# Block products for two more pairs of the second down projection, and DRAM sums for four more units of the second up projection

## The chip, the cores and the metric

The kernel runs on one core of a Trainium2 chip. A core has five engines with queues of their own: TensorE (PE; its weight loads are listed as PEld), VectorE (DVE), ScalarE (ACT), GpSimd (POOL) and SyncE (SP), and 16 DMA engines that all of them feed. The metric is the device time of one execution in microseconds, the median of several runs. Before the change it is 1062.77 us (three runs, 1062.4 to 1063.34).

## The reference

One macaron layer on 512 tokens of 1024 channels, all in float32:

```python
def swiglu(x, w_gate, w_up, w_down):
    return (jax.nn.silu(x @ w_gate) * (x @ w_up)) @ w_down
...
        x = x + 0.5 * swiglu(rmsnorm(x, ffn1_norm[l]), ffn1_wg[l], ffn1_wu[l], ffn1_wd[l])
        x = x + hybrid_mixer(rmsnorm(x, mix_norm[l]), w_in[l], conv_w[l], conv_b[l],
                             rg_wa[l], rg_ba[l], rg_wx[l], rg_bx[l], rg_lam[l],
                             w_att_proj[l], w_rnn_proj[l], w_out[l])
        x = x + 0.5 * swiglu(rmsnorm(x, ffn2_norm[l]), ffn2_wg[l], ffn2_wu[l], ffn2_wd[l])
    return rmsnorm(x, final_norm)
```

The inner width of both feed-forward layers is 2816, that is 22 tiles of 128 rows. The mixer holds sparse attention and a recurrent branch; the change leaves its arithmetic alone.

## The kernel before

**Split precision.** A float32 matrix product is made of three TensorE products: each operand is split into a rounded high part and a remainder (`wsplit`, L238: ACT writes `wh`, DVE writes `wl` as the difference), and high by high, high by low and low by high are added up in PSUM. Nearly every instruction is recorded through one helper, so the profile gives L171 for all of them; tiles tell them apart.

**Stages in order of time.** First up projection, first down projection, mixer (64 jobs of the list `ORDER`, placed by a planner with costs and due times), second up projection, second down projection with the final norm. The two feed-forward stages stand in an order that is written out by hand: events with due times, then a stream of steps.

**Block products.** Two tiles of weights make a two by two block matrix with blocks a11, a12, a21, a22, and seven block products replace eight. They need the sums s1 = a21+a22, s3 = a21+a11, s2 = s1+a11 and s4 = s2+a12 of the weights; the products are numbered 1 (a11), 2 (a12), 3 (s4), 4 (a22), 5 (s1), 6 (s2), 7 (s3). The signs stand in the other operand.

**Second up projection** (`ffn_up`, called with `blocks=BLOCKS2U`). Four tiles of gate and up weights (`DIRECT2`) are multiplied plainly, in eight direct products. The other 18 tiles are 18 units w of seven products each, 126 steps in `stream`. Step i is emitted as `products(i)`, then `step(i)`, which splits the weights of step i+4 (`prepare`, `LEAD` = 4) and reads the results of step i-1. A unit of the plain kind loads its blocks into SBUF slots (`load`), forms s1 and s3 by accumulating DMAs of the POOL queue and s2 and s4 by DVE additions. A unit with an entry in `BLOCKS2U` reads blocks and sums from DRAM: `fetch_pair` loads the weights of two steps into one of three buffers (`RAWS` = 3, tile `wr`). Its sums were formed in DRAM by eight copies and accumulating copies of the POOL queue (class `Blocks`, `stages`). Units 6 to 17 are of this kind (`UNITS` = 6), and all of their seven products are wide: the high weights meet high and low part of the other operand in one 512 column matmul, and one of 256 columns adds the low weights; the halves of the sum are added when the result is read (`copies`, `reads`). Units 0 to 5 have products 2, 5 and 3 wide (`WIDE`), the other four take three matmuls of 256 columns.

**Pace of the DRAM sums.** The sums of the second down projection (`sum_groups`, L1516) are issued between the first mixer jobs, up to the job `SUMS_FROM`; from that job on `sums_until` (L1069) issues those of the second up projection. At each call it records a small DVE `memset` and a POOL copy of it (tile `beat`), so that the POOL queue does not run ahead of DVE. `SUMS_PART` of these moves go out in the mixer, `DIRECT_PART` beside the direct products, the rest over the first `SUMS_STEPS` steps of the stream.

**Second down projection** (`block_down` with its own loop). The 22 hidden tiles are `hs`: the first `PLAIN` = 6 are multiplied plainly, the others form `PAIRS` = 8 pairs (a, b). A step ("D", h, k) multiplies plain tile k for output half h (12 matmuls of 512 columns), a step (p, j) is product p of pair j (6 matmuls of 512 columns). The order of the 68 steps: the six D steps of half 0, products 1, 2, 5 for all pairs, then 6 and 3 with four D steps of half 1 between them, 7, two D steps, 4. Tasks are keyed to steps: the weights of two steps are split four steps ahead (`split_pair`, three `wh`/`wl` buffers), an operand (tile `cm`, two halves) is made some 5 or 6 steps ahead, and `differences(j)` (DVE: tile `cr`, and `h` in place) stands at step j. Tasks of negative steps run beside the last steps of the stream (`ahead`). At steps 0 to 3 `turn` transposes the residual (8 small matmuls each, and four ACT copies to tile `xr`). The results of the D steps of half 0 are added to `xr` by four DVE instructions after step 5.

Of the kernel before, what the change touches and what calls it, by code (L numbers as in the profile page):

```python
# [14 lines left out]
P = 128  # L15
# [161 lines left out]
def hybrid_kernel(ctx, tc, xt, vec, w1u, w1d, wm, wki, wrg, watt, wrnn, wout, w2u, w2d, gf, out):  # L177
# [243 lines left out]

    def ffn_up(y, wu, n0, tiles, hs, g, norm, norm_at, waiting=(), given=(), ahead=None, blocks={}, wide=()):

# [312 lines left out]
        if ahead and waiting:  # L736
            def held(d):
                nc.vector.memset(beat[:, d:d + 1], 0.0)
                nc.gpsimd.tensor_copy(beat[:, d:d + 1], beat[:, d:d + 1])
                ahead(d - 200)  # L740

            for d in range(PAIRS // 2 + 1):
                at(R + 0.7 + 5.4 * d, held, d)
# [30 lines left out]
        with tc.manual_schedule(engines=ENGINES):  # L774
# [9 lines left out]
            for i in range(len(stream)):  # L784
                begin(T0 + i * 1.42)
                products(i)
                step(i)
                if ahead:
                    ahead(i - len(stream))
                if i % 14 == 12 and i // 14 < PLAIN:  # L790
                    halve(hs, i // 14)
                if blocks and i % 2 == 0:
                    sums_until(SUMS_PART + DIRECT_PART + (1 - SUMS_PART - DIRECT_PART) * min(1.0, i / SUMS_STEPS))
                if i % 7 == 1 and loaded[0] < count - len(blocks):
                    load_ = load()
                next(load_, None)
# [12 lines left out]

    def down_blocks(wd):  # L810
        part = lambda b, j: wd[b * (PAIRS // 2) + j // 2][:, j % 2 * S:(j % 2 + 1) * S]
        return [Blocks(*(part(b, j) for b in range(4))) for j in range(PAIRS)]

    def block_down(hs, wd, sums, blocks=None):

# [17 lines left out]
        def block(b, j):  # L833

            i, half = b * (PAIRS // 2) + j // 2, j % 2 * S
            return wd[i][:, half:half + S]
# [3 lines left out]
        def source(i):  # L840
            if steps[i][0] == "D":
                _, h, k = steps[i]
                return wd[2 * PAIRS + h * (PLAIN // 2) + k // 2][:, k % 2 * S:(k % 2 + 1) * S]
            p, j = steps[i]
# [26 lines left out]

        a = lambda j: hs[PLAIN + 2 * j]
        b = lambda j: hs[PLAIN + 2 * j + 1]

# [40 lines left out]
        for i, st in enumerate(steps):  # L915
# [8 lines left out]
            if st[0] == "D":  # L924
                _, h, k = st
                key = ("D", h, k // 2)
                if k % 2 == 0:
                    used.append([i - 4, index["D", h, k + 1] - 4, key, 2 * PAIRS + h * (PLAIN // 2) + k // 2])
                task(i - 4, unit(i, lambda key=key, k=k: raws[key][:, k % 2 * S:(k % 2 + 1) * S]))
                continue  # L930
            p, j = st
            if p in (1, 4, 2):
                key = (p, j // 2)
                if j % 2 == 0:
                    used.append([i - 4, index[p, j + 1] - 4, key, {1: 0, 2: 1, 4: 3}[p] * (PAIRS // 2) + j // 2])
                src = lambda key=key, j=j: raws[key][:, j % 2 * S:(j % 2 + 1) * S]
# [53 lines left out]

        d.steps, d.index, d.tasks, d.tasks_at, d.units, d.turned = steps, index, tasks, tasks_at, units, turned
        return d
# [173 lines left out]
    def products1(i, ms=range(KD // 2)):  # L1166
        h, l = (t[:, i % 2 * S:(i % 2 + 1) * S] for t in d1.units[i // 2])
        if steps[i][0] == "D":
            _, half, k = steps[i]
            hh, hl = hs[k]  # L1170
            for m in ms:
# [4 lines left out]
                T.matmul(o, h[:, c], hl, start=False, stop=False)  # L1176
                T.matmul(o, l[:, c], hh, start=False, stop=k == PLAIN - 1)
            return
        p, j = steps[i]
        t = d1.turned[p, j]  # L1180
        for m in ms:
# [4 lines left out]
            T.matmul(o, h[:, c], t[:, hi], start=False, stop=False, **opens)  # L1186
            T.matmul(o, l[:, c], t[:, lo], start=False, stop=j == PAIRS - 1, **opens)

# [4 lines left out]
    def results1(i):  # L1193
        st = steps[i]
        if st[0] == "D":
            if st[2] == PLAIN - 1:
# [3 lines left out]
        elif st[1] == PAIRS - 1:  # L1200
            for a in ADDS[st[0]]:
# [683 lines left out]
    def products(i, ms=range(2)):  # L1885
        h, l = (t[:, i % 2 * S:(i % 2 + 1) * S] for t in units[i // 2])
        if steps[i][0] == "D":
            _, half, k = steps[i]
            hh, hl = hs[k]
            for m in range(NQ):  # L1890
# [135 lines left out]
def _layout(i):  # L2026
    def blocks(d):

        t = d[0].reshape(KF, P, 2, S)
        pairs = t[PLAIN:].reshape(PAIRS // 2, 2, 2, P, 2, S).transpose(4, 2, 0, 3, 1, 5).reshape(2 * PAIRS, P, 2 * S)  # L2030
        plain = t[:PLAIN].reshape(PLAIN // 2, 2, P, 2, S).transpose(3, 0, 2, 1, 4).reshape(PLAIN, P, 2 * S)
        return np.concatenate([pairs, plain])
# [5 lines left out]
    for n, g in enumerate(("rg_wa", "rg_wx")):  # L2038
# [35 lines left out]
```

## Time and profile before

| | |
|---|---|
| median of three runs | 1062.77 us |
| profiled execution | 1061.5 us |
| its span, first to last instruction | 1059.7 us |
| direct products of the second up projection | about 716 to 762 us |
| its stream of 126 steps | 762.4 to 940.0 us |
| second down projection | 940.0 to about 1052 us, then the last norm and stores |

Times within the span count from its first instruction. In rows of the timeline the columns are start, duration, engine, line, operation, tiles as out<-in, shape and count; in brackets stands the idle time before and what ended it. Matmuls overlap in the array, so the pace of PE is read from the difference of starts and not from durations; the same holds for DVE, where the next instruction starts some 0.09 us before the one ahead of it ends.

### The profile page before, as it was taken

The numbers are of one execution on the slowest core, as the hardware profiler recorded it, in microseconds if no ns is written. First come the engines' busy times: TensorE is split into PE (matmuls) and PEld (weight loads), VectorE is DVE, ScalarE is ACT, GpSimd is POOL, SyncE is SP. The second block draws the span as 40 slices with busy tenths as digits, with TensorE's granted clock in tenths as the row PEclk, the third lists the DMA queues.
The fourth block names the chain that finished last, engine by engine and source line by source line (L and its number), as shares of the span: only waits on it lengthen the run. The fifth ranks groups of instructions, "written<-read, shape, count | busy, mean of one in ns | idle before, by whom it ended". The sixth has DMA issues, their size and how long they took to land.

```text
span 1059.7 us, 16590 instructions
## 1 busy us (share of the span) xinstructions
PE 1051.1 (99%) x5716; PEld 909.6 (86%) x5716; DVE 884.9 (84%) x1742; ACT 667.1 (63%) x1250; POOL 237.2 (22%) x357
## 2 busy tenths in 40 slices
PE   9999999999999999999999999999999999999997
PEld 7889999989999788888888888888899888888885
DVE  6679999989988879999899866865799888878875
ACT  7456656656476657976886664445666666666663
POOL 0261323302131011212031444442732000000020
PEclk9999999999999999999999999999999999999999
DMA  9786999938783477667494878999994666545573
GB/s 326 180 170 159 264 225 231 233 97 236 182 220 122 128 225 171 179 181 188 126 234 123 208 177 198 278 236 261 265 223 100 191 197 197 180 155 167 187 205 122
DMA packets 94548, 205.26 MB, mean 194 GB/s; under 512 B 11776, under 2 KB 18560, under 8 KB 93824
## 3 DMA queue, kind: packets, MB, share of 16 engines
q1 hardware_dynamic: 60720, 136.24, 39.2%
q0 software_dynamic: 33024, 67.13, 32.9%
q8 instruction: 45, 0.74, 0.3%
q10 hardware_dynamic: 720, 0.84, 0.2%
q14 instruction: 39, 0.32, 0.1%
HBM read 194.72 MB, written 48.23 MB: 229 GB/s over the span
## 4 chain that ended last, share of the span: by engine, by line
PE 97%; ACT 1%; DVE 1%; DMA 0%; issue 0%
PE mm L171 68%; PE aux L171 29%; DMA vt<-vec 0%; ACT L171 0%; ACT rl L171 0%; ACT r L171 0%; DVE tu L171 0%; DVE o L171 0%; DVE wl L171 0%; ACT wh L171 0%; DVE tg L171 0%; ACT yh L171 0%; DVE xr L171 0%; DVE sq L171 0%; ACT xc L171 0%
## 5 line engine op out<-in xcount | busy, mean ns | idle before, releaser
L171 DVE TENSOR_TENSOR wl<-wr,wh 128x1024 fp32r<-128x1024 f32 (+2 forms) x233 | 232.2, 1000 | 60.5 <-ACT wh L171 58.8
L171 ACT ACTIVATE wh<-wr 128x1024 fp32r<-128x1024 f32 (+3 forms) x235 | 203.7, 873 | 76.4 <-PE aux L171 24.0
L171 PE MATMUL mm<-cm,wh 128*128 128x256 f32 (+1 forms) x1184 | 240.9, 310 | 0.0
L171 PEld LDWEIGHTS mm<-cm,wh 128*128 128x128 f32 x1184 | 189.3, 191 | 7.3 <-ACT tu L171 0.2
L171 PE MATMUL mm<-cm,wl 128*128 128x256 f32 x736 | 172.5, 282 | 0.0
L171 PE MATMUL mm<-yh,wh 128*128 128x512 f32 (+1 forms) x416 | 163.8, 394 | 0.3 <-ACT i L171 0.2
L171 PE MATMUL mm<-yl,wh 128*128 128x512 f32 (+1 forms) x416 | 162.2, 390 | 0.0
L171 PE MATMUL mm<-yh,wl 128*128 128x512 f32 x408 | 159.2, 390 | 0.0
L171 PEld LDWEIGHTS mm<-cm,wl 128*128 128x128 f32 x736 | 130.0, 190 | 6.1
L171 PE MATMUL aux<-cm,wh 128*128 128x512 f32 (+1 forms) x472 | 122.9, 379 | 0.0
L171 PEld LDWEIGHTS mm<-yh,wh 128*128 128x128 f32 (+1 forms) x416 | 78.0, 187 | 17.1 <-ACT i L171 0.6
L171 PEld LDWEIGHTS mm<-yl,wh 128*128 128x128 f32 (+1 forms) x416 | 77.6, 187 | 15.6 <-DVE yl L171 0.5
L171 PEld LDWEIGHTS mm<-yh,wl 128*128 128x128 f32 x408 | 76.6, 188 | 16.4 <-DVE wl L171 0.2
L171 PEld LDWEIGHTS aux<-cm,wh 128*128 128x128 f32 x472 | 79.7, 189 | 9.4
L171 ACT ACTIVATE wh<-s 128x512 fp32r<-128x512 f32 x96 | 58.8, 625 | 43.3 <-DVE s L171 32.9
L171 DVE TENSOR_TENSOR wl<-s,wh 128x512 fp32r<-128x512 f32 x96 | 65.4, 688 | 14.5 <-ACT wh L171 13.8
L171 PEld LDWEIGHTS aux<-cm,wl 128*128 128x128 f32 x440 | 68.8, 189 | 8.7
L171 PE MATMUL aux<-cm,wl 128*128 128x256 f32 x440 | 74.0, 281 | 0.0
L326 POOL DMA_DIRECT2D scr<-w2d x32 | 29.6, 1003 | 175.5 <-DMA scr<-w2d 163.5
L159 POOL DMA_DIRECT2D s<-w1u x44 | 41.3, 1136 | 114.4 <-DVE wl L171 69.7
L159 POOL DMA_DIRECT2D cm<-h x16 | 13.8, 863 | 207.5 <-ACT cm L171 198.0
L171 PE MATMUL mm<-wh,cm 128*128 128x512 f32 x192 | 59.1, 389 | 0.0
(267 smaller groups left out, 2151.6 us busy)
## 6 DMA issues: line engine op xcount, KB each, us to landing
wr<-scr SPq DMA_DIRECT2D x80, 256.0 KB, 2.9
wr<-wm SPq DMA_DIRECT2D x39, 512.0 KB, 3.9
scr<-w2u POOLq DMA_DIRECT2D x72, 256.0 KB, 6.1
s<-w1u POOLq DMA_DIRECT2D x44, 256.0 KB, 7.6
scr<-scr POOLq DMA_DIRECT2D x40, 256.0 KB, 6.1
wr<-w1u SPq DMA_DIRECT2D x19, 512.0 KB, 6.2
wr<-w1d SPq DMA_DIRECT2D x18, 512.0 KB, 4.2
wr<-w2u SPq DMA_DIRECT2D x36, 256.0 KB, 2.9
```

The lines of the kernel that those rows point to most:

```text
L159: return self.engine.dma_start(out, src, **kw)
L171: return call(*args, **kw)
L326: plain, adds = nc.gpsimd.dma_start, lambda o, i: nc.gpsimd.dma_start(o, i, accum_op=ALU.add)
```

## The change

The constants of the second feed-forward layer part from those of the first.

- `PLAIN2` = 2 and `PAIRS2` = 10 in the second down projection: four of the six plain tiles become two more pairs, so that 74 steps replace 68. No D step of half 1 stands between products 6 and 3 any more; both stand ahead of product 4.
- `UNITS` = 2: units 2 to 5 of the second up projection read their sums from DRAM and become all wide.
- The pace of the sums: 128 moves in place of 96 for the up projection and 80 in place of 64 for the down projection; they begin at job 33 in place of 37, 68% of them go in the mixer, 7% beside the direct products, and the remaining 32 moves over the first 62 steps (before 9 or 10 over 44).

```diff
-PLAIN, PAIRS, TAIL = 6, 8, 3
+PLAIN1, PAIRS1, PLAIN2, PAIRS2, TAIL = 6, 8, 2, 10, 3
...
-UNITS, SUMS_FROM, SUMS_PART, DIRECT_PART, SUMS_STEPS, SUMS_TIME = 6, 37, 0.8, 0.1, 44, 145
+UNITS, SUMS_FROM, SUMS_PART, DIRECT_PART, SUMS_STEPS, SUMS_TIME = 2, 33, 0.68, 0.07, 62, 185
...
-                if i % 14 == 12 and i // 14 < PLAIN:
+                if i % 14 == 12 and i // 14 < halves:
                     halve(hs, i // 14)
...
-        steps = [("D", 0, k) for k in range(PLAIN)] + [(p, j) for p in (1, 2, 5) for j in range(PAIRS)]
+        steps = [("D", 0, k) for k in range(plain)] + [(p, j) for p in (1, 2, 5) for j in range(pairs)]
         for p in (6, 3):
-            for j in range(PAIRS):
-                steps += [(p, j)] + [("D", 1, (6, 3).index(p) * 2 + j // 3)] * (j in (2, 5))
-        steps += [(7, j) for j in range(PAIRS)] + [("D", 1, k) for k in (4, 5)] + [(4, j) for j in range(PAIRS)]
+            for j in range(pairs):
+                steps += [(p, j)] + [("D", 1, (6, 3).index(p) * 2 + j // 3)] * (j in (2, 5) and plain > 2)
+        steps += [(7, j) for j in range(pairs)] + [("D", 1, k) for k in range(plain - 2, plain)] + [(4, j) for j in range(pairs)]
...
-    d2 = block_down(hs, w2d, x, BLOCKS2D)
+    d2 = block_down(hs, w2d, x, PLAIN2, PAIRS2, BLOCKS2D)
...
-    ffn_up(y2, w2u, 0, DIRECT2, hs, V_G2, norm_steps(acc), (2.73, 3.2, 3.4, 4.78, 5.3), ahead=tasks_at, blocks=BLOCKS2U, wide=WIDE)
+    ffn_up(y2, w2u, 0, DIRECT2, hs, PLAIN2, V_G2, norm_steps(acc), (2.73, 3.2, 3.4, 4.78, 5.3), ahead=tasks_at, blocks=BLOCKS2U, wide=WIDE)
```

The other lines hand these numbers on (`PLAIN1` and `PAIRS1` for the first layer, whose values stay 6 and 8) and lay the weights out to match.

On DVE, at the front of the second down projection, from the four results of the plain steps on (tile `xr`). Before:

```order
L171 SCALAR_TENSOR_TENSOR xr_10544<-aux_10560,xr_10544 128x512
L171 SCALAR_TENSOR_TENSOR xr_10544<-aux_10564,xr_10544 128x512
L171 SCALAR_TENSOR_TENSOR xr_10545<-aux_10568,xr_10545 128x512
L171 SCALAR_TENSOR_TENSOR xr_10545<-aux_10572,xr_10545 128x512
L171 TENSOR_TENSOR wl_10760<-wr_10617,wh_10759 128x1024
L171 TENSOR_TENSOR cr_10763<-h_10389,h_10318 128x256
L171 TENSOR_TENSOR h_10389<-h_10389 128x256
L171 SCALAR_TENSOR_TENSOR cm_10766<-h_10389,cm_10766 128x256
L171 TENSOR_TENSOR cm_10769<-cr_10715,cm_10769 128x256
L171 TENSOR_TENSOR cr_10763<-h_10539,h_10503 128x256
L171 TENSOR_TENSOR h_10539<-h_10539 128x256
```

In the same place now:

```order
L171 SCALAR_TENSOR_TENSOR xr_10575<-aux_10591,xr_10575 128x512
L171 SCALAR_TENSOR_TENSOR xr_10575<-aux_10595,xr_10575 128x512
L171 SCALAR_TENSOR_TENSOR xr_10576<-aux_10599,xr_10576 128x512
L171 SCALAR_TENSOR_TENSOR xr_10576<-aux_10603,xr_10576 128x512
L171 TENSOR_TENSOR cr_10680<-h_9118,h_9034 128x256
L171 TENSOR_TENSOR h_9118<-h_9118 128x256
L171 TENSOR_TENSOR wl_10684<-wr_10530,wh_10683 128x1024
L171 SCALAR_TENSOR_TENSOR cm_10687<-h_9994,cm_10687 128x256
L171 TENSOR_TENSOR cm_10690<-cr_10607,cm_10690 128x256
L171 TENSOR_TENSOR cr_10680<-h_9346,h_9266 128x256
L171 TENSOR_TENSOR h_9346<-h_9346 128x256
```

Before, the results follow on the differences of pairs 0 to 5, and those of 6 and 7 come after; now those of pairs 0 and 1 stand ahead and the differences of pairs 2 to 9 come after. The split for steps 6 and 7 (`wl_10684`) stands behind the results, as that for steps 10 and 11 (`wl_10760`) did.

On DVE at the end of the stream, between the last two units' results (tiles `c`, `tu`, `tg`, `e`, `h`) and the first split of the down projection. Before:

```order
L171 TENSOR_TENSOR wl_10488<-wr_10416,wh_10487 128x1024
L171 TENSOR_TENSOR c_10499<-aux_10464,c_10499 128x512
L171 TENSOR_TENSOR tu_10429<-c_10499 128x256
L171 TENSOR_TENSOR h_10503<-tu_10429,tg_10330 128x256
L171 TENSOR_TENSOR e_10369<-aux_10378,e_10369 128x512
L171 SCALAR_TENSOR_TENSOR tg_10329<-e_10369 128x256
L171 TENSOR_TENSOR wl_10519<-wr_10447,wh_10518 128x1024
L171 TENSOR_TENSOR tu_10429<-mm_10403,tu_10429 128x256
L171 TENSOR_TENSOR h_10503<-tu_10429,tg_10330 128x256
L171 TENSOR_TENSOR e_10473<-aux_10464,e_10473 128x512
L171 SCALAR_TENSOR_TENSOR tu_10428<-e_10473 128x256
L171 TENSOR_TENSOR wl_10577<-wr_10476,wh_10576 128x1024
```

In the same place now:

```order
L171 SCALAR_TENSOR_TENSOR cm_10527<-h_8886,cm_10527 128x256
L171 TENSOR_TENSOR e_10388<-aux_10397,e_10388 128x512
L171 SCALAR_TENSOR_TENSOR tg_10348<-e_10388 128x256
L171 TENSOR_TENSOR wl_10544<-wr_10466,wh_10543 128x1024
L171 SCALAR_TENSOR_TENSOR cm_10547<-h_9118,cm_10547 128x256
L171 TENSOR_TENSOR tu_10448<-mm_10422,tu_10448 128x256
L171 TENSOR_TENSOR h_10525<-tu_10448,tg_10349 128x256
L171 SCALAR_TENSOR_TENSOR cm_10562<-h_9346,cm_10562 128x256
L171 TENSOR_TENSOR e_10492<-aux_10483,e_10492 128x512
L171 SCALAR_TENSOR_TENSOR tu_10447<-e_10492 128x256
L171 TENSOR_TENSOR h_10570<-tu_10447,tg_10348 128x512
L171 TENSOR_TENSOR cr_10607<-h_8608,h_8669 128x256
```

Four low halves of operands of product 1 (`cm`, the first of them just ahead of these rows) now stand between the last results of the stream, and the split for steps 4 and 5 moves behind the first difference.

On the POOL queue, in the first steps of the stream. Before, with the additions for the slots of units 2 and 3 (tile `s`) between the moves in DRAM (tile `scr`):

```order
L159 DMA s_1583_8517<-w2u 128x512
L159 DMA s_1584_8518<-w2u 128x512
L1075 COPY beat<-beat 128x1
L326 DMA scr_2837<-w2u 128x512
L1075 COPY beat<-beat 128x1
L1078 DMA scr_2845<-scr_2843 16x4096
L159 DMA s_1607_8653<-w2u 128x512
L159 DMA s_1608_8654<-w2u 128x512
```

Now:

```order
L1075 COPY beat<-beat 128x1
L1078 DMA scr_2863<-scr_2862 16x4096
L1075 COPY beat<-beat 128x1
L326 DMA scr_2870<-w2u 128x512
L1075 COPY beat<-beat 128x1
L326 DMA scr_2872<-w2u 128x512
L1075 COPY beat<-beat 128x1
L326 DMA scr_2845<-w2u 128x512
```

Each `beat` stands for two steps of the stream, and one move follows it nearly every time, up to step 62.

More of the change, by code (lines that the diff above doesn't have):

```diff
@@ L420, in weight_blocks, with ffn_up @@
         return got
-    def ffn_up(y, wu, n0, tiles, hs, g, norm, norm_at, waiting=(), given=(), ahead=None, blocks={}, wide=()):
+    def ffn_up(y, wu, n0, tiles, hs, halves, g, norm, norm_at, waiting=(), given=(), ahead=None, blocks={}, wide=()):
         H = KD // 2 * P
@@ L740, in held @@
                 ahead(d - 200)
-            for d in range(PAIRS // 2 + 1):
+            for d in range(PAIRS1 // 2 + 1):
                 at(R + 0.7 + 5.4 * d, held, d)
@@ L833, in block @@
         def block(b, j):
-            i, half = b * (PAIRS // 2) + j // 2, j % 2 * S
+            i, half = b * (pairs // 2) + j // 2, j % 2 * S
             return wd[i][:, half:half + S]
@@ L842, in source @@
                 _, h, k = steps[i]
-                return wd[2 * PAIRS + h * (PLAIN // 2) + k // 2][:, k % 2 * S:(k % 2 + 1) * S]
+                return wd[2 * pairs + h * (plain // 2) + k // 2][:, k % 2 * S:(k % 2 + 1) * S]
             p, j = steps[i]
@@ L870, in unit @@
             return split_
-        a = lambda j: hs[PLAIN + 2 * j]
-        b = lambda j: hs[PLAIN + 2 * j + 1]
+        a = lambda j: hs[plain + 2 * j]
+        b = lambda j: hs[plain + 2 * j + 1]
         def differences(j):
@@ L927, in block_down @@
                 if k % 2 == 0:
-                    used.append([i - 4, index["D", h, k + 1] - 4, key, 2 * PAIRS + h * (PLAIN // 2) + k // 2])
+                    used.append([i - 4, index["D", h, k + 1] - 4, key, 2 * pairs + h * (plain // 2) + k // 2])
                 task(i - 4, unit(i, lambda key=key, k=k: raws[key][:, k % 2 * S:(k % 2 + 1) * S]))
@@ L989, in tasks_at @@
                 t()
-        d.steps, d.index, d.tasks, d.tasks_at, d.units, d.turned = steps, index, tasks, tasks_at, units, turned
+        d.plain, d.pairs, d.steps, d.index, d.tasks, d.tasks_at, d.units, d.turned = plain, pairs, steps, index, tasks, tasks_at, units, turned
         return d
@@ L1176, in products1 @@
                 T.matmul(o, h[:, c], hl, start=False, stop=False)
-                T.matmul(o, l[:, c], hh, start=False, stop=k == PLAIN - 1)
+                T.matmul(o, l[:, c], hh, start=False, stop=k == PLAIN1 - 1)
             return
@@ L1186, in products1 @@
             T.matmul(o, h[:, c], t[:, hi], start=False, stop=False, **opens)
-            T.matmul(o, l[:, c], t[:, lo], start=False, stop=j == PAIRS - 1, **opens)
+            T.matmul(o, l[:, c], t[:, lo], start=False, stop=j == PAIRS1 - 1, **opens)
     def result1(p, m, s_, half, sign):
@@ L1895, in products @@
                 T.matmul(o, hl[:, c], h, start=False, stop=False)
-                T.matmul(o, hh[:, c], l, start=False, stop=k == PLAIN - 1)
+                T.matmul(o, hh[:, c], l, start=False, stop=k == PLAIN2 - 1)
             return
@@ L1904, in products @@
             T.matmul(o, tl, h, start=False, stop=False, **opens)
-            T.matmul(o, th, l, start=False, stop=j == PAIRS - 1, **opens)
+            T.matmul(o, th, l, start=False, stop=j == PAIRS2 - 1, **opens)
     def rows(m, half):
@@ L2026, in _layout, with blocks @@
 def _layout(i):
-    def blocks(d):
+    def blocks(d, n, m):
         t = d[0].reshape(KF, P, 2, S)
-        pairs = t[PLAIN:].reshape(PAIRS // 2, 2, 2, P, 2, S).transpose(4, 2, 0, 3, 1, 5).reshape(2 * PAIRS, P, 2 * S)
-        plain = t[:PLAIN].reshape(PLAIN // 2, 2, P, 2, S).transpose(3, 0, 2, 1, 4).reshape(PLAIN, P, 2 * S)
+        pairs = t[n:].reshape(m // 2, 2, 2, P, 2, S).transpose(4, 2, 0, 3, 1, 5).reshape(2 * m, P, 2 * S)
+        plain = t[:n].reshape(n // 2, 2, P, 2, S).transpose(3, 0, 2, 1, 4).reshape(n, P, 2 * S)
         return np.concatenate([pairs, plain])
```

32 lines of the change are left out of this document (16 added, 16 removed).

## The prediction

> **What bounds the kernel now.** I read the page first: its span, the busy times, the chain that ended last.
>
> ```profile
> span 1059.7 us, 16590 instructions
> ...
> PE 1051.1 (99%) x5716; PEld 909.6 (86%) x5716; DVE 884.9 (84%) x1742; ACT 667.1 (63%) x1250; POOL 237.2 (22%) x357
> ...
> PE 97%; ACT 1%; DVE 1%; DMA 0%; issue 0%
> ```
>
> TensorE bounds it: 97% of the chain is matmuls. A saving on PE counts in full as long as nothing that feeds PE comes late, and a lost microsecond of PE is a lost microsecond of the kernel. So I next read how near the feeders are, in busy time by stretch (PE, PEld, DVE, ACT, POOL, then PE's clock, DMA share and rate).
>
> ```profile
> 820.00:940.00 120.00, 120.00 (x690) 105.09 (x689) 102.91 (x153) 76.48 (x114) 1.31 (x2) 1.00 0.62 193
> 940.00:956.00 16.00, 16.00 (x89) 13.62 (x88) 11.57 (x24) 10.91 (x29) 0.00 (x0) 1.00 0.31 101
> 956.00:974.00 18.00, 18.00 (x81) 14.91 (x80) 17.86 (x35) 9.94 (x20) 0.00 (x0) 1.00 0.51 162
> 974.00:996.00 22.00, 22.00 (x98) 18.20 (x97) 18.27 (x36) 16.12 (x30) 0.00 (x0) 1.00 0.63 197
> ```
>
> At the front of the second down projection DVE is busy 17.86 of 18 us (956 to 974). PE does not stop there only because of a head start that DVE got beside the six plain steps before (11.57 of 16 us). The change takes four of those six steps away, so this is where I look for the answer.
>
> **What PE saves.** Starts of PE instructions, in the stream and in the down projection:
>
> ```profile
> 769.49 0.40 PE L171 MATMUL mm<-cm,wh 128*128 128x256 f32 x2
> ...
> 770.93 1.09 PE L171 MATMUL aux<-cm,wh 128*128 128x512 f32 x4
> ...
> 772.33 1.09 PE L171 MATMUL aux<-cm,wh 128*128 128x512 f32 x4
> ...
> 940.02 0.27 PE L171 MATMUL mm<-ident,x 128*128 128x128 f32 x1
> ...
> 943.66 1.03 PE L171 MATMUL mm<-ident,x 128*128 128x128 f32 x8
> ...
> 947.27 1.03 PE L171 MATMUL mm<-ident,x 128*128 128x128 f32 x8
> ...
> 957.25 0.39 PE L171 MATMUL aux<-wh,hh 128*128 128x512 f32 x1
> ...
> 959.97 0.62 PE L171 MATMUL mm<-wh,cm 128*128 128x512 f32 x2
> ...
> 970.85 0.62 PE L171 MATMUL aux<-wh,cm 128*128 128x512 f32 x2
> ```
>
> - Stream: a narrow product takes 770.93 - 769.49 = 1.44 us, a wide one 772.33 - 770.93 = 1.40. Units 2 to 5 turn four narrow products each into wide ones: 16 x 0.04 = 0.6 us.
> - Down projection: a plain step takes 959.97 - 957.25 = 2.72 us, a pair's product (970.85 - 959.97) / 8 = 1.36. Eight plain steps go, 21.76 us; two pairs of seven products come, 19.04. That is 2.7 us.
>
> PE saves 3.3 us. I hold this for nearly sure: the counts are in the code, and the rates are steady.
>
> **What the front of the down projection gives back.** DVE's rows there:
>
> ```profile
> 936.15 1.23 DVE L171 TENSOR_TENSOR wl<-wr,wh 128x1024 fp32r<-128x1024 f32 x1 [1.43 <-ACT wh L171]
> ...
> 942.51 0.43 DVE L171 SCALAR_TENSOR_TENSOR tu<-e 128x256 f32<-128x256 f32 x1
> 942.86 1.22 DVE L171 TENSOR_TENSOR wl<-wr,wh 128x1024 fp32r<-128x1024 f32 x1
> 943.99 0.69 DVE L171 TENSOR_TENSOR h<-tu,tg 128x512 f32<-128x512 f32 x1
> 944.59 0.42 DVE L171 TENSOR_TENSOR cr<-h,h 128x256 f32<-128x256 f32 x1
> ...
> 959.72 2.47 DVE L171 SCALAR_TENSOR_TENSOR xr<-aux,xr 128x512 f32<-128x512 f32 x4
> 962.12 1.21 DVE L171 TENSOR_TENSOR wl<-wr,wh 128x1024 fp32r<-128x1024 f32 x1
> 963.25 0.42 DVE L171 TENSOR_TENSOR cr<-h,h 128x256 f32<-128x256 f32 x1
> 963.70 0.42 DVE L171 TENSOR_TENSOR h<-h 128x256 f32<-128x256 f32 x1
> 964.04 0.41 DVE L171 SCALAR_TENSOR_TENSOR cm<-h,cm 128x256 fp32r<-128x256 f32 x1
> 964.38 0.42 DVE L171 TENSOR_TENSOR cm<-cr,cm 128x256 fp32r<-128x256 f32 x1
> 964.71 0.42 DVE L171 TENSOR_TENSOR cr<-h,h 128x256 f32<-128x256 f32 x1
> ```
>
> From start to start: a result (xr) (962.12 - 959.72) / 4 = 0.60 us, a split (wl) 1.13, the two differences of a pair 964.04 - 963.25 = 0.79, an operand's low half (cm) 0.335.
>
> When does DVE begin the differences? Now at 944.59, behind the last result of the stream. The changed order puts four operand halves ahead, 4 x 0.335 = 1.34 us; the last of these results needs the tu begun at 942.51, 0.455 after its start by the like pair of dependent rows (963.25 to 963.70), and the split of 942.86 moves behind. So 942.51 + 1.34 + 0.455 + 0.60 = 944.9. DVE's idle time ahead of 936.15 cannot take the four up, since they stand behind that split in the queue.
>
> What must DVE do until PE may start the fifth product of kind 2, step 16? Seven splits (steps 4 to 17), ten pairs' differences, 6 operand halves of product 1, 10 of product 7 and 5 of product 2, four results of the plain steps, two of product 1: 7 x 1.13 + 10 x 0.79 + 21 x 0.335 + 6 x 0.60 = 26.5 us. The last split ends at 944.9 + 26.5 + 0.1 = 971.5.
>
> When does PE want it? The stage starts at 940.02; two plain steps with transposes end at 947.27; two products with transposes take 1.36 + (3.61 - 2.72) = 2.25 each (3.61 from 943.66 to 947.27), up to 951.8; twelve more products take 16.3, up to 968.1. The low weights are first read by the third matmul, 0.45 later: 968.5. PE waits 971.5 - 968.5 = **3.0 us** in all, spread over steps 10 to 16 in waits for wl of 0.5 to 1 us, with every later matmul queued behind. After that DVE needs 1.8 us for a pair of product 2 (one split, two halves) against PE's 2.72 and gets ahead again. From both sides: 0.9 us is the least, as the next rows show; 4 us if the results of the plain steps come late too.
>
> ```profile
> 941.80 0.68 DVE L171 TENSOR_TENSOR e<-aux,e 128x512 f32<-128x512 f32 x1
> ...
> 942.97 0.39 PE L171 MATMUL aux<-wh,hh 128*128 128x512 f32 x1
> ```
>
> The fourth plain chain opens the PSUM bank that this e read frees. It ends at 942.48, 0.5 us before PE comes; 1.34 us later it ends at 943.82, and PE waits 0.85 us. That wait lies inside the 3.0 (PE then comes 0.85 us later to steps for which it would wait anyway), but it stays if DVE should keep up later.
>
> [...]
>
> **Edits that I cost at nothing.**
>
> ```profile
> 520.00:600.00 80.00, 80.00 (x372) 66.48 (x371) 76.86 (x168) 58.56 (x109) 17.82 (x31) 1.00 0.63 165
> ...
> L1074 DVE MEMSET beat<- x62: 59/59/59, 573.1 to 822.4; 128x1 f32 x62
> ...
> 996.00:1041.00 45.00, 45.00 (x200) 37.27 (x199) 32.95 (x51) 23.63 (x44) 6.91 (x8) 1.00 0.69 190
> ```
>
> - 25 more beats cost DVE 25 x 0.06 = 1.5 us, spread over the mixer's second half and the stream. PE runs on there with DVE at 76.86 of 80 us; without that cover some 0.5 us.
> - DVE and ACT in the stream from 762 to 820: the additions of s2 and s4 go, wide reads come. At worst it is as in the stretch 820 to 940, where DVE has 102.91 of 120 us and PE never stops.
> - Products 6 and 3 lose the four plain steps between them, the cover under DVE's 32.95 of 45 us. Now 20 products at 1.36 us, 27.2 us, stand over two halves and half a split each (1.24 us) and four results: 27.1 us. DVE enters with some 3 us of lead, so I take nothing; 1 us if that lead is gone.
>
> **The sum.** 1061.5 (the profiled execution) - 3.3 + 3.0 = 1061.2 us, 0.3 below its own time. The median stands 1.27 above that execution, so 1062.77 - 0.3 = **1062.5 us**.
>
> **Rival, slower: the pair loads starve.** In the first 62 steps every two steps bring one DRAM move beside the loads of the weights, where the stretch 820 to 940 had nearly the loads alone.
>
> ```profile
> 716.00:762.00 46.00, 46.00 (x211) 38.23 (x210) 32.09 (x64) 25.52 (x52) 24.66 (x36) 1.00 1.00 259
> ...
> q0 software_dynamic: 3325, 8.60, 55.2%
> ...
> scr<-w2u POOLq DMA_DIRECT2D x29, 256.0 KB, 5.8
> scr<-scr POOLq DMA_DIRECT2D x4, 256.0 KB, 5.6
> ...
> wr<-w2u SPq DMA_DIRECT2D x5, 512.0 KB, 6.6
> ...
> 978.99 1.06 ACT L171 ACTIVATE wh<-wr 128x1024 fp32r<-128x1024 f32 x1 [1.05 <-PE aux L171]
> ...
> 980.08 1.23 DVE L171 TENSOR_TENSOR wl<-wr,wh 128x1024 fp32r<-128x1024 f32 x1 [0.82 <-ACT wh L171]
> ```
>
> Between 573 and 640 us 33 moves took 55.2% of 67 us, 1.12 us of all DMA engines each; one in 2.81 us is a share of 0.40. Loads alone stand at 0.62. The sum, 1.02, has no room: 0.02 of 87 us is 1.7 us. If loads land as wr did from 640 to 716 (6.6 us beside such moves), a buffer turns round in 6.6 + 2.3 (from 978.99 until the split ends at 981.31), three buffers give a pair of steps in 2.97 us against 2.81, and some 24 pairs lose 0.16 us each: 3.8 us, 1066.3. It decides from a landing of about 6.1 us on. For it: 259 GB/s at a share of 1.00 between 716 and 762, where 193 + 93 = 286 are wanted. Against it: the units' own slot loads and additions, which fill the queues today, are gone, and the splits run some 3 us ahead of PE. [...] Chance 0.27.
>
> **Rival, faster: DVE keeps up.** If the splits came 2 us earlier than my queue has them, only the wait for the PSUM bank would stay: 1062.77 - 3.3 + 0.85 = 1060.3. For it speaks that PE never stopped at this place before; against it that DVE has no idle time left in the 26.5 us and that its rows are steady to 0.01 us. Chance 0.17.
>
> **How the numbers follow.** This kernel's measurement tells apart about 0.2%, 2.1 us. Forecast with its own range 1061 to 1064.5 (0.53), starving loads (0.27), DVE keeping up (0.17), 0.03 for a new stall elsewhere. The range takes in the bank wait alone at the low end and the starved loads at the high end: 1060.2 to 1066.6.
>
> **What would show it.** Right: PE idle behind wl of the down projection, some 3 us between 950 and 968 us, DVE without a gap there, product 2 reached about 6 us earlier in the stage than now, and the last matmul at about the same time. Wrong: no PE wait there (then faster), or waits of PE or of ACT's wh for wr in the stream between 775 and 850 us with landings over 6 us (then slower).

## The result, and the profile after

The changed kernel takes **1072.87 us** (median of five runs, 1071.33 to 1073.87) against 1062.65 us before (five runs, 1062.40 to 1063.34). The ratio is 1.0096, 95% interval 1.0082 to 1.0110: about 10 us slower, and 6 us above the upper end of the forecast range. The profiled execution took 1073.44 us.

The head of its page, with the same lines as before:

```profile
span 1071.5 us, 16594 instructions
...
PE 1053.5 (98%) x5640; PEld 903.9 (84%) x5640; DVE 892.7 (83%) x1769; ACT 674.3 (63%) x1256; POOL 267.0 (25%) x420
...
PE 86%; DVE 5%; DMA 4%; ACT 3%; issue 2%; SPq 0%; POOL 0%; ACTq 0%; DVEq 0%; POOLq 0%
```

The chain that ended last was 97% matmuls; now it is 86%, and DVE, DMA and ACT share most of the rest. PE waits for its feeders. Three places in PE's timeline of the profiled executions part the span into stages: the first matmul of the stream, the first transpose of the second down projection, and the last matmul. Before:

```profile
762.37 0.40 PE L171 MATMUL mm<-cm,wh 128*128 128x256 f32 x2
...
1052.23 0.39 PE L171 MATMUL mm<-wl,cm 128*128 128x512 f32 x1
```

After:

```profile
763.03 0.40 PE L171 MATMUL mm<-cm,wh 128*128 128x256 f32 x2
...
947.12 0.60 PE L171 MATMUL mm<-ident,x 128*128 128x128 f32 x4
...
1064.16 0.39 PE L171 MATMUL mm<-wl,cm 128*128 128x512 f32 x1
```

With the 940.02 us of before (shown in the prediction), the stream took 177.65 us and takes 184.09; the down projection took 112.21 us and takes 117.04. The 11.8 us that the span grew are 0.66 ahead of the stream (762.37 to 763.03), 6.44 in the stream and 4.83 in the down projection; the tail after the last matmul took 7.5 us and takes 7.3. Against what their matmuls alone should have needed (177.05 and 109.5 us, by the savings of 0.6 and 2.7), the stream lost 7.0 us and the down projection 7.5.

The waits in the stream (the view of waits of the changed kernel, 775 to 870 us: who waited for whom, us in all, times, longest), and the busy time of 785 to 870 us by stretch, whose columns are those of the prediction:

```profile
ACT wh L171 <- DMA wr<-scr: 16.0, 11, 3.2
...
ACT wh L171 <- DMA wr<-w2u: 11.1, 8, 3.0
...
PE mm L171 <- ACT c L171: 2.6, 3, 1.0
PE mm L171 <- ACT e L171: 2.5, 2, 1.5
```

Before:

```profile
785.00:870.00 85.00, 85.00 (x540) 76.87 (x540) 75.39 (x133) 52.44 (x89) 10.52 (x17) 1.00 0.58 155
```

After:

```profile
785.00:870.00 85.00, 79.93 (x447) 68.59 (x447) 66.02 (x121) 48.73 (x73) 22.70 (x52) 1.00 0.93 252
...
950.00:971.50 21.50, 20.70 (x103) 16.86 (x101) 21.12 (x45) 14.70 (x36) 0.00 (x0) 1.00 0.39 125
1003.00:1041.00 38.00, 35.85 (x150) 27.26 (x149) 30.36 (x52) 25.36 (x52) 8.56 (x10) 1.00 0.77 200
```

Before, PE was busy 85.00 of the 85 us from 785 to 870; now it is 79.93, and each of its waits is for `c` or `e`, copies that ACT makes of sums in PSUM; none is for split weights. At 950 DVE has no gap (21.12 of 21.5 us), as forecast. At 1003 it has one: DVE is idle for 7.6 of 38 us while PE waits. That was not forecast.

### The profile page after: what moved, and what is told of

Its sections match the earlier page's. It is cut to its first block, busy times and chain, and to the rows that moved or that the text cites. A ratio compares the mean times of both kernels' runs of the same rounds, so it can differ in the third digit from the quotient of the medians.

```text
span 1071.5 us, 16594 instructions
## 1 busy us (share of the span) xinstructions
PE 1053.5 (98%) x5640; PEld 903.9 (84%) x5640; DVE 892.7 (83%) x1769; ACT 674.3 (63%) x1256; POOL 267.0 (25%) x420
## 4 chain that ended last, share of the span: by engine, by line
PE 86%; DVE 5%; DMA 4%; ACT 3%; issue 2%; SPq 0%; POOL 0%; ACTq 0%; DVEq 0%; POOLq 0%
PE mm L171 63%; PE aux L171 23%; DVE wl L171 2%; DMA wr<-scr 2%; ACT wh L171 1%; DMA wr<-w2u 1%; DVE h L171 1%; DVE cm L171 1%; DMA scr<-w2u 0%; DVE tu L171 0%; DMA wr<-w1u 0%; DVE xr L171 0%; ACT L171 0%; DVE tg L171 0%; ACT rl L171 0%
## 5 line engine op out<-in xcount | busy, mean ns | idle before, releaser
L171 DVE TENSOR_TENSOR wl<-wr,wh 128x1024 fp32r<-128x1024 f32 (+2 forms) x247 | 250.6, 1018 | 64.4 <-ACT wh L171 59.0
L171 ACT ACTIVATE wh<-wr 128x1024 fp32r<-128x1024 f32 (+3 forms) x249 | 219.3, 886 | 88.7 <-DMA wr<-scr 20.0
L171 PE MATMUL mm<-cm,wh 128*128 128x256 f32 (+1 forms) x1120 | 235.8, 319 | 5.1 <-ACT c L171 2.6
L171 PEld LDWEIGHTS mm<-cm,wh 128*128 128x128 f32 x1120 | 180.3, 191 | 15.2 <-ACT c L171 3.6
L171 PE MATMUL mm<-cm,wl 128*128 128x256 f32 x736 | 164.5, 282 | 0.0
L326 POOL DMA_DIRECT2D scr<-w2d x40 | 38.6, 1098 | 166.6 <-DMA scr<-w2d 136.5
L171 PE MATMUL mm<-wh,cm 128*128 128x512 f32 x240 | 74.3, 391 | 0.0
L171 ACT ACTIVATE wh<-s 128x512 fp32r<-128x512 f32 x80 | 48.9, 626 | 36.5 <-DVE s L171 26.2
L1075 POOL COPY beat<-beat 128x1 f32<-128x1 f32 x87 | 31.9, 366 | 142.8 <-DVE beat L1074 132.2
L171 DVE TENSOR_TENSOR wl<-s,wh 128x512 fp32r<-128x512 f32 x80 | 54.8, 690 | 14.4 <-ACT wh L171 13.7
```

Of the source, the lines that this page charges most:

```text
L171: return call(*args, **kw)
L326: plain, adds = nc.gpsimd.dma_start, lambda o, i: nc.gpsimd.dma_start(o, i, accum_op=ALU.add)
L1075: nc.gpsimd.tensor_copy(paces[-1], paces[-1])
```

## The experiments

All ran with several rounds against the kernel before on the same chip; its median there was 1061.8 to 1062.3 us. The lengths are read from the profiled execution of each as above; the streams of e5, e8, e10, e11 and e12, in which PE hardly waits, agree within 0.3 us (176.8 to 177.1).

| kernel | median us | ratio to before (95%) | stream starts at | stream | down projection |
|---|---|---|---|---|---|
| before | 1062.65 | 1 | 762.4 | 177.6 | 112.2 |
| changed | 1072.87 | 1.0096 (1.0082 to 1.0110) | 763.0 | 184.1 | 117.0 |
| e1 up alone | 1069.02 | 1.0074 (1.0052 to 1.0096) | 764.6 | 187.1 | 112.2 |
| e2 down alone | 1066.77 | 1.0045 (1.0030 to 1.0060) | 763.5 | 177.6 | 116.6 |
| e3 slow sums | 1070.37 | 1.0074 (1.0046 to 1.0101) | 762.8 | 184.0 | 117.2 |
| e4 early sums of operands | 1068.20 | 1.0057 (1.0040 to 1.0074) | 762.8 | 184.0 | 112.6 |
| e5 four buffers | 1067.99 | 1.0058 (1.0043 to 1.0073) | 764.6 | 177.1 | 116.3 |
| e6 moves in the mixer | 1074.64 | 1.0116 (1.0101 to 1.0131) | 763.6 | 183.0 | 116.8 |
| e7 down repaired | 1064.08 | 1.0019 (1.0010 to 1.0029) | 763.1 | 177.6 | 113.9 |
| e8 all repairs | 1064.94 | 1.0029 (1.0017 to 1.0040) | 764.1 | 177.1 | 114.0 |
| e9 down spread | 1061.19 | 0.9990 (0.9981 to 1.0000) | 763.0 | 177.6 | 111.3 |
| e10 few moves in the stream | 1067.02 | 1.0040 (1.0027 to 1.0054) | 763.6 | 177.1 | 116.9 |
| e11 combined | 1060.93 | 0.9984 (0.9975 to 0.9993) | 763.4 | 176.8 | 111.3 |
| e12 combined, product 7 earlier | 1061.10 | 0.9989 (0.9980 to 0.9998) | 763.4 | 177.1 | 110.5 |

### Each half of the change alone

e1, the up projection alone:

```diff
-PLAIN1, PAIRS1, PLAIN2, PAIRS2, TAIL = 6, 8, 2, 10, 3
+PLAIN1, PAIRS1, PLAIN2, PAIRS2, TAIL = 6, 8, 6, 8, 3
```

> Only the second up projection and the pace of its sums are changed; the second down projection stays at six plain tiles and eight pairs. In the changed kernel the stages part like this: the stream of 126 steps took about 7 us longer than it should, the second down projection about 7 us longer than its matmuls. If the stages lose apart from each other, this kernel keeps the loss of the stream alone: 1062.65 - 0.6 + 7 = about 1069 us, with PE idle in the stream between 775 and 870 us. Rival: the moves for the down projection's two more pairs (16 more in the mixer) shift the stream's moves and are part of its loss; then it loses clearly less than 7 us, 1063 to 1066 us.

e2, the down projection alone:

```diff
-UNITS, SUMS_FROM, SUMS_PART, DIRECT_PART, SUMS_STEPS, SUMS_TIME = 2, 33, 0.68, 0.07, 62, 185
+UNITS, SUMS_FROM, SUMS_PART, DIRECT_PART, SUMS_STEPS, SUMS_TIME = 6, 37, 0.8, 0.1, 44, 145
```

> Only the second down projection is changed (two plain tiles, ten pairs); the up projection and the pace of its sums are those of before. Theory: front wait behind wl 2.6 us and the waits of products 6, 3 and 7 some 3.5 us, against 2.7 us of matmuls saved: 1062.65 + 3.4 = about 1066 us. Rival: the waits of the down projection come from the late stream (its loads and operands arrive late behind it); then they are gone here and the time is 1062.65 - 2.7 = 1060 us.

The halves are apart. e1 has the loss of the stream and a down projection of 112.2 us, that of before; e2 has the stream of before and a down projection of 116.6 us. Each rival falls. The loss of the stream is uneven: e1's runs took 1068.03 to 1073.59 us, and its profiled one was the longest (2 us of that lie at the very start: its first transposes of the norms stand at 30.6 us). Its longest wait of PE, 2.14 us at 870 us, was followed by a lower granted clock (the column after POOL):

```profile
875.00:880.00 5.00, 5.00 (x25) 4.25 (x25) 4.90 (x9) 2.60 (x3) 0.00 (x0) 0.80 0.48 153
```

The two wide products after that wait took 2.11 and 2.34 us from start to start (872.85, 874.96, 877.30), in place of 1.40. So this run's loss is larger than its waits. e2's runs took 1066.55 to 1067.16.

### The stream: how much is moved, or when a load lands

e3 spreads the last 32 moves over more steps:

```diff
-UNITS, SUMS_FROM, SUMS_PART, DIRECT_PART, SUMS_STEPS, SUMS_TIME = 2, 33, 0.68, 0.07, 62, 185
+UNITS, SUMS_FROM, SUMS_PART, DIRECT_PART, SUMS_STEPS, SUMS_TIME = 2, 33, 0.68, 0.07, 104, 185
```

> The changed kernel with its last 32 moves spread over 104 steps of the stream in place of 62. Theory (moves and loads together fill the DMA engines): a move each 3.25 steps is a share of 0.24 beside 0.62, under 0.9, so that the loads land in 3 to 4 us, PE's waits in the stream go nearly whole, and the time falls by some 6 us to about 1067. Rival (the all-wide reads of units 2 to 5 make ACT and DVE late, whatever the moves do): the waits between 775 and 870 us stay, within 1 us of 1072.9.

Neither came. The four runs took 1065.61 to 1073.24 us, and the profiled one, at 1073.24 the longest, has a stream as long as the changed kernel's with DMA engines that are less full:

```profile
785.00:870.00 85.00, 81.70 (x463) 70.86 (x463) 68.38 (x119) 51.36 (x77) 15.12 (x34) 1.00 0.81 226
```

A share of 0.81 and still 3.3 us of waits in this stretch: fullness does not explain it. By itself this run decides nothing, as its times spread over 7.6 us. But its loads point to the slow landings: shortest, median and longest landing of all pair loads (`wr`) issued from 785 to 865 us, first in the changed kernel, then in e3:

```profile
DMA to landing us min/median/max: 2.7/5.3/7.2
```

```profile
DMA to landing us min/median/max: 2.5/4.4/6.8
```

The median fell by 0.9 us and the longest hardly, and the stream lost as much (184.0 us).

e5 leaves moves and loads as they are and adds a buffer:

```diff
-SLOTS = 60
+SLOTS = 58
...
-    raw = ctx.enter_context(tc.tile_pool(name="raw", bufs=RAWS))
+    raw = ctx.enter_context(tc.tile_pool(name="raw", bufs=RAWS + 1))
...
-                    fetch_pair(i + 2 * RAWS)
+                    fetch_pair(i + 2 * RAWS + 2)
...
-                fetch_pair(even + 2 * RAWS)
+                fetch_pair(even + 2 * RAWS + 2)
```

> The changed kernel with a fourth buffer wr for the pairs of weights in the stream (two slots fewer elsewhere), each pair fetched two steps earlier. Moves and loads are the same. Theory: a load that is issued beside a move lands in 5 to 7 us, and three buffers leave it about 6.1; a fourth gives 2.8 us more (8.9), so ACT's wh hardly waits for wr any more, PE's waits in the stream (6 us of the 10) fall below 1.5 us: about 1067 us (ratio to before 1.0045). Rival 1 (the DMA engines lack throughput): the delay adds up over the 62 steps whatever the depth, so the loss falls by less than 3 us. Rival 2 (the wide reads make ACT and DVE late): no change, 1.0096.

e10 keeps three buffers and leaves 13 moves of 32 in the stream:

```diff
-UNITS, SUMS_FROM, SUMS_PART, DIRECT_PART, SUMS_STEPS, SUMS_TIME = 2, 33, 0.68, 0.07, 62, 185
+UNITS, SUMS_FROM, SUMS_PART, DIRECT_PART, SUMS_STEPS, SUMS_TIME = 2, 33, 0.86, 0.04, 100, 185
```

> The changed kernel with 86% of the moves in the mixer, 4% beside the direct products and the last 13 over 100 steps of the stream (32 over 62 in the changed kernel). Theory: a stall needs a pair's loads to fall beside a move; with 13 moves in place of 32 the stream, 184.1 us in the changed kernel and 177.1 with a fourth buffer, takes 177 to 180 us, and fewer moves beside the direct products leave the operands' transfers on time (they cost 3.9 us when all moves were done before the stream): 1072 - 5 = about 1067 us, ratio 1.005. Rival: any move in the stream beside three buffers costs about 0.2 us, so that 13 cost 2.8 us, and the mixer loses 1 us or more: ratio 1.007.

e6 leaves none there (`SUMS_PART, DIRECT_PART = 0.9, 0.1`):

> The changed kernel with all 128 moves done before the stream (90% in the mixer, 10% beside the direct products). Theory: without a move in the stream the loads land in about 3 us as they do after 870 us, and the 6 us of PE's waits in the stream go; what the mixer loses by 28 more moves is open (its waits are to be read in the trace); if nothing, ratio 1.004, about 1066.5 us. Rival (the wide reads of units 2 to 5): the waits between 775 and 870 us stay although no move runs.

The same stretch in e5, e10 and e6, one fence each:

```profile
785.00:870.00 85.00, 85.00 (x487) 74.31 (x486) 74.29 (x136) 54.94 (x80) 22.89 (x52) 1.00 0.96 275
```

```profile
785.00:870.00 85.00, 84.91 (x485) 74.18 (x484) 73.94 (x118) 54.07 (x79) 7.08 (x16) 1.00 0.69 210
```

```profile
785.00:870.00 85.00, 85.00 (x481) 74.44 (x482) 69.75 (x102) 53.66 (x79) 0.00 (x0) 0.98 0.54 177
```

PE is full in all three. e5 is the one that decides: DMA engines at 0.96 and 275 GB/s, fuller than in the changed kernel (0.93, 252), and no wait of PE. So the DMA engines can carry loads and moves; what was missing was time between the issue of a load and its use. The median landing of the loads in this stretch (issues, 785 to 865 us), in the changed kernel, e5, e10 and e6:

```profile
wr<-scr SPq DMA_DIRECT2D x32, 256.0 KB, 5.3
```

```profile
wr<-scr SPq DMA_DIRECT2D x34, 256.0 KB, 5.5
```

```profile
wr<-scr SPq DMA_DIRECT2D x34, 256.0 KB, 3.5
```

```profile
wr<-scr SPq DMA_DIRECT2D x32, 256.0 KB, 2.9
```

Without moves a load lands in 2.9 us, with 13 of them in 3.5, with 32 in 5.3; e5's loads land no sooner (5.5) and ACT's wh no longer waits for any of them. The longest landing was 7.2 us in the changed kernel and 7.5 in e5, but 4.8 in e10 and 4.9 in e6. One stall of the changed kernel in the chain of waits (start, us, what) shows how a late load reaches PE:

```profile
796.73 0.32 SPq L159
...
797.11 6.98 DMA wr<-scr
...
804.19 0.47 ACT wh L171
804.66 0.49 issue
805.15 0.61 ACT hh L171
805.77 0.49 ACT c L171
...
806.30 0.73 PE mm L171 x2
```

The load took 6.98 us. ACT waited for it with wh, and behind wh in ACT's queue stood `c`, the copy of a finished sum out of PSUM; PE needed that bank and stopped. It did not run out of split weights. That the additions and reads of the wide units had made ACT and DVE late (the rival of these runs) falls too: e5 and e10 have the same reads.

e6 was no faster than the changed kernel all the same (1.0116 beside 1.0096, with intervals that overlap). Its chain of waits at the start of the stream:

```profile
768.58 6.44 DMA scr<-scr
...
775.57 0.52 POOL scr L326
776.08 0.55 POOL cm L159
776.64 8.09 DMA cm<-cq
784.73 0.04 issue
784.77 0.80 PE mm L171 x2
```

In the changed kernel's trace POOL issues the moves and the small transfers that finish the operands (cm), SP the loads; ACT issues five transfers in all, PE and DVE none. In e6 the moves beside the direct products stand in the POOL queue ahead of those of cm: by the chain, a move (775.57) waited for the landing of an earlier one, and the last cm stood behind it. That transfer took 8.09 us, which is not long by itself; before, the median of the same four transfers was 9.3 us, and PE waited for none. What changed is when they were issued, at the latest at 766.8 us in the changed kernel and at 776.6 in e6 (the second of the two times in the rows below). In order: the landing before, the issues in the changed kernel, the issues in e6.

```profile
cm<-cq POOLq DMA_DIRECT2D x4, 128.0 KB, 9.3
```

```profile
L159 POOL DMA_DIRECT2D cm<-cq x4: 1412/1715/1837, 762.9 to 766.8; - x4
```

```profile
L159 POOL DMA_DIRECT2D cm<-cq x4: 1098/1256/1492, 771.2 to 776.6; - x4
```

PE waited 2.33 and 1.23 us for these transfers, and then ran at a lower granted clock for a while:

```profile
785.00:790.00 5.00, 5.00 (x25) 4.52 (x26) 3.09 (x6) 2.37 (x5) 0.00 (x0) 0.69 0.06 21
```

So the stream comes to 183.0 us again, for another reason than in the changed kernel.

### The down projection: DVE's time, or a ring of waits

e4 makes two DVE subtractions earlier and changes nothing else:

```diff
-                task(i - before - 1, lambda j=j: V.tensor_sub(a(j)[:, lo], b(j)[:, hi], a(j)[:, hi]))
+                task(i - before - 1 - 2 * (blocks is not None), lambda j=j: V.tensor_sub(a(j)[:, lo], b(j)[:, hi], a(j)[:, hi]))
...
-                task(i - before - 1, lambda j=j: V.tensor_sub(a(j)[:, lo], b(j)[:, lo], a(j)[:, lo]))
+                task(i - before - 1 - 2 * (blocks is not None), lambda j=j: V.tensor_sub(a(j)[:, lo], b(j)[:, lo], a(j)[:, lo]))
```

> The changed kernel with the DVE differences that form the operands of products 6 and 4 (h from h and h) two steps earlier. Theory: in products 6, 3 and 7 a ring of ACT's wh, DVE's wl, cm and h and ACT's cm turns once in 3.33 us where PE needs 2.72 for two steps; two steps of lead cut the ring, and the 3 to 3.5 us of PE's waits between 1003 and 1040 us go: about 1069.5 us. Rival: DVE simply has too much to do there (27.1 of 27.2 us by the prediction); then the order doesn't matter, and the time stays within 1 us of 1072.9.

The down projection falls from 117.0 to 112.6 us, by more than the 3 to 3.5 us expected. In the stretch in which PE lost 2.15 us in the changed kernel it now waits for nothing, and DVE did more there, not less:

```profile
1003.00:1041.00 38.00, 38.00 (x169) 31.48 (x168) 31.79 (x52) 25.64 (x51) 8.66 (x10) 1.00 0.80 229
```

The ring that e4 cuts, one turn in the chain of waits of the changed kernel, at product 6:

```profile
1008.49 1.23 DVE wl L171
1009.71 0.34 DVE cm L171
1010.05 0.35 DVE h L171
...
1010.42 0.02 ACT cm L171
...
1010.74 1.05 ACT wh L171
...
1011.82 1.24 DVE wl L171
```

From wl to wl 3.33 us, where two steps of PE take 2.72. DVE's `h` stands behind wl; ACT's `cm`, half of the next operand, needs this h; ACT's next wh stands behind that cm; DVE's next wl needs that wh. No engine is full (in the row of 1003 to 1041 us above PE has 35.85, DVE 30.36 and ACT 25.36 of 38 us), and the ring sets the pace.

e7 applies e4's edit to the down projection alone and moves the work of the front back by eight steps:

```diff
-                task(j, differences(j))
-            before = {1: 6, 6: 6, 7: i - j - 1, 4: i - index[3, j]}.get(p, 5)
+                task(j + 8 * (blocks is not None), differences(j))
+            before = {1: 6, 6: 6, 7: i - j - 1 - 8 * (blocks is not None), 4: i - index[3, j]}.get(p, 5)
```

> The down projection's change alone (as in the second run, 1.0045 of before), with the two differences (h for products 6 and 4) two steps earlier and differences(j) and the operands of product 7 eight steps later, from the front to the steps of products 2 and 5, where DVE needs 1.8 us for two steps and PE 2.72. Theory: both of its waits go but the 0.9 us for the PSUM bank at the first plain step: 1061.8 - 2.7 + 0.9 = 1060.0 us, ratio 0.9983. Rival (DVE lacks time over the whole of products 1, 2 and 5): the waits move to products 2 and 5, about 2 us stay, ratio 1.000 to 1.001.

The rival was nearer, and the time came out above it too (1.0019): the front is free but for the bank wait (0.9 us), and waits of 2.8 us stand at products 2 and 5, where DVE now has 16.76 of 17 us:

```profile
965.00:982.00 17.00, 14.72 (x62) 11.01 (x61) 16.76 (x39) 10.55 (x23) 0.00 (x0) 1.00 0.39 135
```

My figure of 1.8 us for two steps did not count what I moved there: two pairs' differences (1.58) and two operand halves of product 7 (0.67) bring it to 4.05 us against 2.72.

e8 puts e5 and e7 together:

> The whole change with the fourth buffer and both repairs of the down projection. If the causes add up: 3.3 us of matmuls saved, 0.9 us of the bank wait and up to 1.5 us of rest in the stream: 1061.8 - 3.3 + 0.9 + 1 = about 1060.4 us, ratio 0.9987. If the stream's loss is throughput, 1064 us or more, ratio over 1.002.

The time (1064.94 us) lies where the expectation put a lack of throughput. The stages say otherwise: the stream took 177.1 us, so the fourth buffer did its work, and the miss stands in the down projection (114.0 us, as in e7) and in a late start. The stream also starts 1.7 us later than before; in e5 it is 2.2. Both have two slots fewer and a wait of 1.2 us and one of 0.4 at 654 us in the mixer that no other run shows. That the slots cause it was not tried by itself.

e9 spreads the same work evenly, with the down projection alone:

```diff
-                task(j, differences(j))
-            before = {1: 6, 6: 6, 7: i - j - 1, 4: i - index[3, j]}.get(p, 5)
+                task(5 * j // 2 + 1 if blocks else j, differences(j))
+            before = {1: (3 if j < 2 else 4) if blocks else 6, 6: 6, 7: i - 2 * j - 12 if blocks else i - j - 1, 4: i - index[3, j]}.get(p, 5)
```

> The down projection's change alone, with h for products 6 and 4 two steps earlier as before, but the differences spread evenly (pair j at step 5j/2 + 1), the operands of product 7 at step 2j + 12, and product 1's operands 3 or 4 steps ahead in place of 6, so that one of their halves in place of four stands in the stream's tail. DVE then has about 2.7 us of work for each two steps, PE 2.72. Theory (the waits are DVE's backlog at one place, and there is room if it is spread): both waits go, also the 0.9 us for the PSUM bank; from the first transpose to the last matmul 109.5 to 110.5 us (112.2 before, 116.6 with the change alone, 113.9 with all of it eight steps later); 1061.8 - 2.7 + 0.5 = about 1059.6 us, ratio 0.998. Rival (there is no room at all in these 32 steps): some 3 us of waits stay, ratio 1.000 or more.

The waits of the front go, the bank wait too, since three of the four operand halves no longer stand ahead of the e read. One wait of 1.2 us is left at product 6, where the operands of product 7 meet h of product 6 and the results of product 5. The down projection takes 111.3 us, where 109.5 to 110.5 were expected; with a ratio of 0.9990 (0.9981 to 1.0000) the kernel cannot be told from before.

### Together

e11 has e9's order and e10's pace:

> The whole change with the spread of the down projection and the pace of 13 moves in the stream. If the parts add up: 1061.8 - 3.3 + 0.5 + 1 to 3 = 1060 to 1062 us, ratio 0.998 to 1.000; if the spread has no room, 1063 or more.

e12 makes the operands of product 7 five steps earlier (`i - 2 * j - 7`):

> As the combined kernel (0.9984 of before), with the operands of product 7 five steps earlier (step 2j + 7), since DVE's queue had 1.4 to 2.1 us in hand in product 2 and fell 1.6 us behind at product 6, where these operands, h of product 6 and the results of product 5 meet. Theory: the last wait of 1.2 us goes, 110 us from the first transpose to the last matmul in place of 111.3: ratio 0.9970 to 0.9978. Rival: the wait moves forward to product 2 with its size, ratio 0.998 to 0.999.

e11 takes 1060.93 us, 0.9984 of before (0.9975 to 0.9993): faster than both kernels, if by little. e12 halves the last wait (1.2 to 0.6 us) and shortens the down projection to 110.5 us, but its time cannot be told from e11's, and the ratio of 0.9970 to 0.9978 that was expected did not come.

## Why the prediction was wrong, step by step

**What PE saves: right.** Where its waits are gone the stream takes 177.1 us against 177.6 (e5, e8, e10): 0.5 us, forecast 0.6. The down projection comes to 110.5 us with 0.6 us of waits left (e12), so at least 2.3 of the forecast 2.7 us are there.

**The front of the down projection: right, nearly to the number.** I had the last of the seven splits end at 971.5, 31.5 us after the stage's start at 940.02. The changed kernel's chain and timelines at that place:

```profile
977.52 1.15 DVE wl L171
```

```profile
950.99 0.50 PE L171 MATMUL aux<-wh,hh 128*128 128x512 f32 x1 [0.75 <-DVE e L171]
...
972.10 0.50 PE L171 MATMUL aux<-wl,cm 128*128 128x512 f32 x1 [0.66 <-DVE wl L171]
...
975.38 0.50 PE L171 MATMUL aux<-wl,cm 128*128 128x512 f32 x1 [0.25 <-DVE wl L171]
```

It ended at 978.67, 31.55 us after 947.12. The loss is 3.1 us (e4, which has only this one left: 112.6 against 109.5), forecast 3.0; the bank wait for the read of e took 0.9 from start to start (0.75 of it idle in the row above), forecast 0.85. Adding starts to starts, and not durations, was the better way: with the rows' durations (1.22 us for a split, 0.84 for a pair's differences, 0.42 for an operand half) the list comes out 2.9 us longer (7 x 0.09 + 10 x 0.05 + 21 x 0.085), and the estimate of the wait would have been 5.9 us. Only the waits began two steps later than I had put them.

**Products 6 and 3: wrong.** The step reads: "Products 6 and 3 lose the four plain steps between them, the cover ... so I take nothing; 1 us if that lead is gone." They and product 7 lose 4.4 us (117.0 to 112.6 in e4). I counted DVE's work, 27.1 of 27.2 us, and a lead of 3 us; but DVE was not the bound: in the stretch of these waits it is idle for 7.6 of 38 us, and e4 removes the waits with more DVE work in it. The bound was a ring of instructions on two engines, 3.33 us a turn against 2.72, and no sum of busy time shows it. The trace of before did show one turn of it, in its timeline:

```profile
998.03 1.22 DVE L171 TENSOR_TENSOR wl<-wr,wh 128x1024 fp32r<-128x1024 f32 x1
...
1001.35 1.23 DVE L171 TENSOR_TENSOR wl<-wr,wh 128x1024 fp32r<-128x1024 f32 x1 [0.52 <-ACT wh L171]
```

From 998.03 to 1001.35 are 3.32 us, with DVE idle for wh. PE did not wait then. The code of before has a plain step of 2.72 us after the third and the sixth step of each of these two products, which I take for the reason; no run tried it alone. I took away the cover and named it, but read only busy time under it.

**The stream: the rival came, and was priced too low.** It had a chance of 0.27 and 3.8 us; the stream lost 7.0. The mechanism was in it: a load that is issued beside a move comes late (a median of 5.3 us with 32 moves over 62 steps, 2.9 with none in e6), and three buffers cannot wait. Two of its numbers failed. First, the sum of shares, 0.40 + 0.62 = 1.02, "has no room": e5 ran the same transfers at 275 GB/s without a wait of PE, so the 259 GB/s at a share of 1.00 between 716 and 762 us were no ceiling. There was room, and the loss came all the same, by landing times. Second, "It decides from a landing of about 6.1 us on": the median landing was 5.3, under that point, and the loss was nearly twice the price. (The 6.6 us that the rival used stood in a row of 512 KB loads; those of the stream bring 256 KB.) Single loads took up to 7.2 us, and one in the chain above 6.98. With three buffers, the runs whose longest landing passed 6.1 us (changed 7.2, e1 7.3, e3 6.8) lost 7 us or more in the stream; in e10 and e6, at 4.8 and 4.9, PE hardly waited from 785 to 870 us. The late load of that chain held up ACT's queue, where the copy that frees a PSUM bank stood behind wh: on its way from 797.11 to 804.09, `c` begun at 805.77, PE on again at 806.30. I had only looked at the splits.

**The sum.** In place of -3.3 + 3.0 it is -3.3 + 3.1 + 4.4 + 7.0 = 11.2 us, beside 11.8 in the spans; the other 0.66 us are there from the start, as the first transposes of the norms show (28.5 and 29.1 us, the first of the two times in the rows below), ahead of everything that the change touches. In the other runs this time lies between 28.4 (e8) and 30.6 us (e1); why was not tried. Before and after:

```profile
L171 PE MATMUL aux<-ident,rs x12: 271/272/273, 28.5 to 724.2; 128*128 128x128 f32 x12
```

```profile
L171 PE MATMUL aux<-ident,rs x12: 271/272/273, 29.1 to 724.8; 128*128 128x128 f32 x12
```

The range left out that the stream and the ring could both come: each rival was added to the forecast alone.

## What to carry to other kernels

When a change takes slack away, look in the trace of before for rings: follow a wait of one engine to the instruction that it waits for, and what that one stands behind, until you come back; compare one turn with the pace of the bound engine (here 3.33 us against 2.72), since busy time did not show it here (DVE idle for 7.6 of 38 us). Judge prefetch by the slowest landings against the time that the buffers give, not by the mean and not by the share of the DMA engines (here 7.2 us against an estimate of 6.1, at a median of 5.3 and a share of 0.93); one buffer more, or fewer transfers beside the loads, tells which it is. Where two independent risks stand behind a forecast, the range must reach to both together.

## What the runs showed of the hardware that was not expected

The landing of a 256 KB load depended strongly on what ran beside it: a median of 2.9 us with no move (e6), 3.5 with 13 moves spread over 100 steps (e10), 5.3 with 32 over 62 (changed), although DMA still had bandwidth to give (252 GB/s in the changed kernel, 275 in e5). The longest landings were 4.9, 4.8 and 7.2 us.

Some waits of PE were followed by a lower granted clock and cost more than themselves. After 2.14 us (e1) the clock was 0.80 from 875 to 880 us, and two wide products took 2.11 and 2.34 us in place of 1.40; after 2.33 and 1.23 us with three matmuls between them (e6) it was 0.69 from 785 to 790 us. After e3's longest wait of 1.92 us it stayed at 1.00, as it did in the changed kernel, whose longest in the stream was 1.5 us. What decides between these was not tried.
